# The first norm's factor and offset multiplied into the modulation rows during the mixer, on two partitions, instead of on full tiles at its end

## The chip, the cores and the metric

The kernel runs on one core of a Trainium2 chip. The metric is the time of one execution in microseconds of device time; lower is better. PE is TensorE, DVE is VectorE, ACT is ScalarE, POOL is GpSimd, and SP is SyncE, which here only issues DMAs.

## The reference, cut to what matters

One step of a two-layer diffusion backbone with 128 context tokens and 256 latent tokens of 1024 channels. Each layer has a token mixer (convolution, attention and spatial gating, merged and projected) and a mixture of experts. Both are modulated by rows that come from the conditioning, and each is followed by a layer norm:

```python
def trunk_layer(x, cvec, w_ada, b_ada, mix_params, ln1_g, ln1_b, moe_params, ln2_g, ln2_b, ctx_k, ctx_v):
    m = (jax.nn.silu(cvec) @ w_ada + b_ada)[:, None, :]
    sh1, sc1, g1, sh2, sc2, g2 = jnp.split(m, 6, axis=-1)
    mix, k, v = token_mixer(x * (1 + sc1) + sh1, *mix_params, ctx_k, ctx_v)
    x = layer_norm(ALPHA * x + g1 * mix, ln1_g, ln1_b)
    y = hier_moe(x * (1 + sc2) + sh2, *moe_params)
    x = layer_norm(ALPHA * x + g2 * y, ln2_g, ln2_b)
    return x, k, v
```

The change concerns the input of `hier_moe`. With n the normalised value before factor and offset, it is (n * ln1_g + ln1_b) * (1 + sc2) + sh2, which is n * G + B with G = ln1_g * (1 + sc2) and B = ln1_b * (1 + sc2) + sh2. There are two sets of modulation rows: one for the latent tokens (s = 0) and one for the context tokens (s = 1).

## The kernel before

All 384 tokens are worked on together, as three tiles of 128. For each layer the mixer (`mixer`) walks through 72 pieces of 128x1024 weights, n = 0 to 71. A piece is loaded by SP, split into a high and a low part (ACT line 102 and DVE line 110; a few of the low parts on POOL, also line 110), and multiplied three times on PE, high by high, high by low and low by high (lines 97 to 99, or 488 to 490 for the last pieces). Beside the pieces run side steps, written as generators: the convolution (line 505 on DVE, 31 taps), the gating, the attention in four pairs of heads, and the modulation (`ada`). One step of each is traced per piece.

`ada(l, g)` works out 2048 of the 6144 modulation columns. Its matmuls (line 219) are spread over four steps, one in every fourth piece, with a `yield` after each. Two more steps follow: ACT copies the result, and then it is transposed to columns for other uses (lines 229 to 231), the bias is added (line 243, DVE, 128x512, of which only two partitions in each 32 hold rows), for g = 2 one is added to the scale rows (line 245), and four DMAs on POOL's queue store the rows to the tensor `m_d` in HBM (line 247, 4 KB each). g = 1 gives the gate rows g1 and the shift rows sh2, g = 2 the scale rows sc2 and the gate rows g2. In layer 0 the steps of g = 1 begin at piece 5 and those of g = 2 at piece 21; the last step of g = 2 is traced around piece 34. `br` is a table with the biases in the same layout.

The program is ordered by a planner, which simulates the engines and lays down the order of the instructions on each; only stretches marked as a manual schedule keep the order of the text. Each engine, SP and POOL with their DMA issues among them, then works through its own instructions in that order and waits at the first one whose input is missing.

At the end of the mixer `open_ln1` opens new buffers and loads rows, broadcast over 128 partitions, from SP's queue (lines 889 to 893): g1, the norm's factor `lg` and offset `lb`, and sc2 and sh2 for both sets. Then three products and sums of 128x1024 follow on POOL for each set, line 911 (sc * lb), line 912 (sh + that) and line 913 (sc * lg), so that `rows["sc2.."]` holds G and `rows["sh2.."]` holds B. `lg` and `lb` themselves are used once more, far behind, in `affine` (line 1596).

The output projection of the mixer, pieces 64 to 71, runs at the same time. For each block of 256 columns and each token tile, `ln1_part` multiplies by g1 (line 946, DVE), adds the residual (line 949, DVE) and takes the norm's statistics (line 952, DVE); `logit_tr` transposes the result on PE (line 963) and `logit_mm` multiplies it with the router's weights (line 970). In `last_col` the norm is ended: `mean` (line 999, DVE) multiplies by G and `bias` (line 1002, DVE) adds B. Routing and the experts follow. Line 839 (DVE) is the merge of the first branch: it reads the result of a piece from PSUM and so gives the bank back to PE. Line 621 (POOL) turns the queries by the cosine in the attention, and line 599 (POOL) is a product of the gating branch. Line 332 is the load of a piece or of expert weights.

Of the kernel before, what the change touches and what calls it, by code (L numbers as in the profile page):

```python
# [8 lines left out]
F32 = mybir.dt.float32  # L9
# [5 lines left out]
ALU = mybir.AluOpType  # L15
# [5 lines left out]
D = 1024  # L21
# [58 lines left out]
class Kern:  # L80
# [130 lines left out]
    def ada(self, l, g):  # L211

        nc, a = self.nc, self.a
        ps = self.bank("ms")
        for kp in range(4):
            for k in range(2):
                w = self.get(("a", l, g, kp, k))
                for t in range(4):
                    nc.tensor.matmul(ps[32 * t:32 * t + 32, :], self.cT[:, 2 * kp + k, :],  # L219
                                     w[:, t * 512:t * 512 + 512],  # L220
                                     start=(kp == 0 and k == 0), stop=(kp == 3 and k == 1))
                self.done()
            yield
        sb = self.mix.tile([128, 512], F32, tag="tmp", name="adasb", bufs=3)
        self.act(sb, ps, AF.Copy)
        yield
        p2 = self.bank("ms")
        for j in range(4):
            nc.tensor.transpose(p2[:, j * 128:(j + 1) * 128], sb[:, j * 128:(j + 1) * 128], self.ident)
        mT = self.mT[l]  # L230
        nc.vector.tensor_tensor(
            mT[:, g * 16:(g + 1) * 16, :].rearrange("p (t j) s -> p j t s", j=4),
            p2.rearrange("p (j t r) -> p j t r", j=4, t=4)[:, :, :, 0:2],
            self.bT[:, l, g * 16:(g + 1) * 16].rearrange("p (t j) -> p j t", j=4)
            .unsqueeze(3).to_broadcast([128, 4, 4, 2]),
            op=ALU.add)
        if g != 1:
            j = 8 if g == 0 else 32
            nc.vector.tensor_scalar(mT[:, j:j + 8, :], mT[:, j:j + 8, :], 1.0, None, op0=ALU.add)
        if g > 0:  # L240
            br = self.mix.tile([128, 512], F32, tag="tmp", name="adabr", bufs=3)
            nc.sync.dma_start(br, a["badar"][l * 2 + g - 1])
            nc.vector.tensor_tensor(sb, sb, br, op=ALU.add)
            if g == 2:
                nc.vector.tensor_scalar(sb[0:64, :], sb[0:64, :], 1.0, None, op0=ALU.add)
            for t in range(4):
                nc.gpsimd.dma_start(self.m_d[l][g - 1, :, t * 512:(t + 1) * 512], sb[32 * t:32 * t + 2, :])
        yield
# [627 lines left out]
    def open_ln1(self, l):  # L876
        nc, a = self.nc, self.a
        self.pools.close()
        self.pools = ExitStack()
        P = lambda name, **k: self.pools.enter_context(self.tc.tile_pool(name=f"{name}{l}", reuse_waits="tile", **k))  # L880
        self.wx = P("wx", bufs=4)
        self.mo = P("mo", bufs=1)
        self.lpools = ExitStack()
        self.lp = self.lpools.enter_context(self.tc.tile_pool(name=f"lp{l}", bufs=1, reuse_waits="tile"))
        self.route_consts(l)
        rows = self.rows = {}
        md = self.m_d[l]

        def load(name, src, pool):
            t = pool.tile([128, 1024], F32, tag=name if pool is self.lp else "row", name=name, bufs=1 if pool is self.lp else 2)  # L890
            nc.sync.dma_start(t, src.to_broadcast([128, 1024]))
            rows[name] = t
            return t

        self.r = self.hp.tile([128, NT, D], F32, tag="H", name="r1")
        for s in (1, 0):
            load(f"g1{s}", md[0, s:s + 1, 0:1024], self.lp)
        xs = [self.wx.tile([128, 2, D], F32, tag="wx", name="xs") for _ in range(2)]
        self.xs = [xs[0][:, 0], xs[0][:, 1], xs[1][:, 0]]
        src = a["x"] if l == 0 else self.x_d  # L900
        nc.sync.dma_start(xs[0], src[0:256, :].rearrange("(i p) c -> p i c", p=128))
        nc.sync.dma_start(xs[1][:, 0], src[256:T, :])
        g = load("lg", a["ln"][l * 4:l * 4 + 1, :], self.mo)
        b = load("lb", a["ln"][l * 4 + 1:l * 4 + 2, :], self.mo)
        for s in range(2):
            load(f"sc2{s}", md[1, s:s + 1, 0:1024], self.lp)
            load(f"sh2{s}", md[0, s:s + 1, 1024:2048], self.lp)
        for s in range(2):
            sc, sh = rows[f"sc2{s}"], rows[f"sh2{s}"]
            t = self.lp.tile([128, D], F32, tag="t", name="rtmp", bufs=2)  # L910
            nc.gpsimd.tensor_tensor(t, sc, b, op=ALU.mult)  # L911
            nc.gpsimd.tensor_tensor(sh, sh, t, op=ALU.add)
            nc.gpsimd.tensor_tensor(sc, sc, g, op=ALU.mult)
        self.st1 = self.sm.tile([128, NT, 4, 6], F32, tag="st1", name="st1", bufs=1)

    def route_consts(self, l):
# [1056 lines left out]
```

## Time and profile before

| | before |
|---|---|
| median of 3 runs | 1128.73 us (1127.07 to 1132.06) |
| the profiled execution | 1127.33 us, span 1125.6 us |
| PE busy | 1011.2 us, 90% |
| DVE busy | 810.7 us, 72% |
| ACT busy | 417.4 us, 37% |
| POOL busy | 269.7 us, 24% |

The span runs from the first to the last instruction of the profiled execution; the time is a little longer. Layer 0's mixer lies at about 0 to 405 us and layer 1's at about 600 to 950 us, each followed by its experts. Busy shares are means over all of it; what a single edit is worth is read from the waits in its own stretch. In the views a wait is given in brackets behind the instruction that waited, with what ended it.

### The profile page before, as it was taken

What the parts mean: (1) busy time and instruction counts of PE and PEld (TensorE: products, weight loads), DVE (VectorE), ACT (ScalarE), POOL (GpSimd) and SP (SyncE); (2) the same over time, 40 slices, a digit from 0 to 9 for tenths busy, and PEclk for the clock granted to TensorE, in tenths of its full rate; (3) what the DMA queues carried; (4) which work ended last, traced back from release to release, by engine and by line L of the source; (5) the groups of instructions that cost most, each with busy time, mean ns of one, the idle gap of its engine ahead of it and who ended that gap; (6) DMA issues with size and microseconds to landing.
All of it is one profiled execution on the core that took longest, in us unless ns stands there. A gap on an engine that the chain in (4) does not pass through costs nothing. (4 is left out here: it accounts for less than half of the span.)

```text
span 1125.6 us, 20806 instructions
## 1 busy us (share of the span) xinstructions
PE 1011.2 (90%) x8182; PEld 840.7 (75%) x8182; DVE 810.7 (72%) x1530; ACT 417.4 (37%) x753; POOL 269.7 (24%) x232
## 2 busy tenths in 40 slices
PE   7999999999999999776689998999999999778673
PEld 5898978877999988433259897788999998754322
DVE  4399999965446986762569999997834587777437
ACT  4324254434333324341163443445532341434221
POOL 0001431221100510333244043114111025013335
PEclk9999999999999989897989999999999999989888
DMA  9967668447436667799585756773223666689955
GB/s 358 412 241 257 266 217 294 178 163 270 151 112 246 259 262 293 303 420 403 219 315 201 280 217 233 251 290 127 110 94 132 224 244 229 227 317 416 419 204 194
DMA packets 55101, 282.75 MB, mean 251 GB/s; under 512 B 8060, under 2 KB 12284, under 8 KB 27857
## 3 DMA queue, kind: packets, MB, share of 16 engines
q1 hardware_dynamic: 49632, 270.01, 63.1%
q0 software_dynamic: 5360, 11.29, 2.7%
q8 instruction: 69, 1.13, 0.4%
q14 instruction: 40, 0.32, 0.1%
HBM read 262.13 MB, written 24.71 MB: 255 GB/s over the span
## 5 line engine op out<-in xcount | busy, mean ns | idle before, releaser
L97 PE MATMUL ps_mm<-hThi,wr 128*128 128x384 f32 x672 | 229.9, 343 | 4.4 <-ACT hThi L102 2.3
L110 DVE TENSOR_TENSOR wr<-w_raw,wr 128x1024 fp32r<-128x1024 f32 x124 | 162.2, 1309 | 92.4 <-ACT wr L102 92.3
L98 PE MATMUL ps_mm<-hTlo,wr 128*128 128x384 f32 x672 | 228.0, 340 | 0.6 <-DVE hTlo L441 0.4
L99 PE MATMUL ps_mm<-hThi,wr 128*128 128x384 f32 x672 | 227.5, 339 | 0.6 <-DVE wr L110 0.6
L102 ACT ACTIVATE wr<-w_raw 128x1024 fp32r<-128x1024 f32 x140 | 147.5, 1055 | 68.1 <-PE ps_mm L99 37.8
L505 DVE SCALAR_TENSOR_TENSOR cacc<-pad,par,cacc 128x399 f32<-128x399 f32 x240 | 169.2, 705 | 4.2
L97 PEld LDWEIGHTS ps_mm<-hThi,wr 128*128 128x128 f32 x672 | 127.1, 189 | 18.2 <-issue 4.0
L98 PEld LDWEIGHTS ps_mm<-hTlo,wr 128*128 128x128 f32 x672 | 127.1, 189 | 6.3 <-DVE hTlo L441 2.5
L99 PEld LDWEIGHTS ps_mm<-hThi,wr 128*128 128x128 f32 x672 | 127.2, 189 | 2.5 <-DVE wr L110 0.9
L110 POOL TENSOR_TENSOR wr<-w_raw,wr 128x1024 fp32r<-128x1024 f32 x10 | 24.5, 2447 | 201.6 <-ACT wr L102 201.2
L1458 POOL DMA_INDIRECT y_d<-ys,dst x28 | 28.4, 1016 | 172.3 <-DVE hv L1400 73.3
L1446 PE MATMUL ps_sc<-w,hidT 128*32 128x512 f32 x256 | 43.1, 766 | 28.6 <-ACT ys L102 21.9
L1415 PE MATMUL ps_mm<-hv,win 128*32 128x128 f32 x1024 | 46.4, 277 | 9.2 <-DVE hv L1400 7.8
L1400 DVE COPY hv<-w_raw 128x512 f32 x60 | 41.9, 737 | 16.6 <-PE ps_mm L1415 10.8
L1415 PEld LDWEIGHTS ps_mm<-hv,win 128*32 128x32 f32 x1024 | 35.8, 112 | 22.7 <-DVE hv L1400 12.0
L1409 PE MATMUL ps_mm<-w_raw,win 128*32 128x256 f32 x640 | 47.8, 391 | 3.5 <-ACT win L102 3.5
L219 PE MATMUL ps_ms<-w_raw,cT 128*32 128x512 f32 x320 | 48.7, 612 | 1.4 <-DMA w_raw<-in_wada 1.4
L102 ACT ACTIVATE gate<-ps_mm 128x384 f32<-128x384 f32 x40 | 19.6, 490 | 81.6 <-PE ps_mm L99 80.5
L1446 PEld LDWEIGHTS ps_sc<-w,hidT 128*32 128x32 f32 x256 | 8.2, 123 | 45.8 <-ACT ys L102 32.9
L911 POOL TENSOR_TENSOR rtmp<-sc,lb 128x1024 f32<-128x1024 f32 x4 | 9.8, 2478 | 121.8 <-DMA lb<-in_ln 121.8
L842 POOL TENSOR_TENSOR merged<-merged,gate 128x384 f32<-128x384 f32 x16 | 18.1, 1135 | 87.0 <-DVE gate L841 87.0
L102 ACT ACTIVATE win<-xT 128x256 f32 x64 | 21.5, 409 | 37.6 <-PE ps_mm L1409 30.2
(505 smaller groups left out, 2355.7 us busy)
## 6 DMA issues: line engine op xcount, KB each, us to landing
w_raw<-in_wst SPq DMA_DIRECT2D x68, 1024.0 KB, 6.4
w_raw<-in_wada SPq DMA_DIRECT2D x48, 1024.0 KB, 5.4
w_raw<-in_w SPq DMA_DIRECT2D x40, 1024.0 KB, 10.7
w<-in_w SPq DMA_DIRECT2D x32, 1024.0 KB, 12.3
w_x<-in_w SPq DMA_DIRECT2D x24, 1024.0 KB, 11.8
bias<-in_bias SPq DMA_DIRECT2D x8, 768.0 KB, 7.6
y_d<-zero SPq DMA_DIRECT2D x2, 3072.0 KB, 15.1
yy<-y_d SPq DMA_DIRECT2D x6, 1024.0 KB, 7.1
```

Source lines behind the costliest of these rows:

```text
L97: mm(out, whi, xhi, start=first, stop=False)
L98: mm(out, whi, xlo, start=False, stop=False)
L99: mm(out, wlo, xhi, start=False, stop=last)
L102: return self.nc.scalar.activation(out, in_, f, **k)
L110: (eng or self.nc.vector).tensor_tensor(lo, x, hi.bitcast(F32), op=ALU.subtract)
L219: nc.tensor.matmul(ps[32 * t:32 * t + 32, :], self.cT[:, 2 * kp + k, :], w[:, t * 512:t * 512 + 512], start=(kp == 0 and k == 0), stop=(kp ...
L505: nc.vector.scalar_tensor_tensor(acc, pad[:, j:j + W], w, acc, op0=ALU.mult, op1=ALU.add)
L1400: nc.vector.tensor_copy(hv[:, i, :], src)
L1409: nc.tensor.matmul(ps[e * 32:(e + 1) * 32, 0:256], x[:, k, e * 32:(e + 1) * 32], w[:, e, kk, :], start=k == 0, stop=k == 7, skip_group_che ...
L1415: nc.tensor.matmul(ps[t * 32:(t + 1) * 32, 256:384], x[:, k, 128 + i * 32:160 + i * 32], hv[:, i, kk, h * 128:(h + 1) * 128], start=False, ...
L1446: nc.tensor.matmul(po[e * 32:(e + 1) * 32, :], hT[:, e * 32:(e + 1) * 32], w2[:, e, :], start=True, stop=True)
L1458: ins = nc.gpsimd.indirect_dma_start(out=view, out_offset=bass.IndirectOffsetOnAxis(ap=dst, axis=0), in_=rows, in_offset=None, bounds_chec ...
```

## The change

The three products and sums on POOL for each set, lines 907 to 913, are taken out of `open_ln1`. In their place `ada` works out G and B for g = 2 before the rows are stored. When g = 2 begins, three buffers of 64x512 are taken, and six DMAs from POOL's queue load the norm's factor and offset (each row to two partitions) and the shift rows that g = 1 stored. In its last step, four matmul steps later, DVE does six instructions of 2x512, B = lb * sc + sh and G = sc * lg for each half of the 1024 channels, and POOL's queue stores B over the shift rows in `m_d`. The stores of the scale rows then carry G. The loads in `open_ln1` are the same as before and bring G and B.

```diff
--- before.py
+++ after.py
@@ -211,6 +211,14 @@
     def ada(self, l, g):
 
         nc, a = self.nc, self.a
+        if g == 2:
+            lg, lb, sh = (self.mix.tile([64, 512], F32, tag="lnr", name="lnr", bufs=3) for _ in range(3))
+            for t in range(2):
+                c = slice(t * 512, (t + 1) * 512)
+                r = slice(32 * t, 32 * t + 2)
+                for k, x in enumerate((lg, lb)):
+                    nc.gpsimd.dma_start(x[r, :], a["ln"][l * 4 + k:l * 4 + k + 1, c].to_broadcast([2, 512]))
+                nc.gpsimd.dma_start(sh[r, :], self.m_d[l][0, :, 1024 + t * 512:1024 + (t + 1) * 512])
         ps = self.bank("ms")
         for kp in range(4):
             for k in range(2):
@@ -242,7 +250,14 @@
             nc.sync.dma_start(br, a["badar"][l * 2 + g - 1])
             nc.vector.tensor_tensor(sb, sb, br, op=ALU.add)
             if g == 2:
+
                 nc.vector.tensor_scalar(sb[0:64, :], sb[0:64, :], 1.0, None, op0=ALU.add)
+                for t in range(2):
+                    r = slice(32 * t, 32 * t + 2)
+                    nc.vector.tensor_tensor(lb[r, :], lb[r, :], sb[r, :], op=ALU.mult)
+                    nc.vector.tensor_tensor(lb[r, :], lb[r, :], sh[r, :], op=ALU.add)
+                    nc.vector.tensor_tensor(sb[r, :], sb[r, :], lg[r, :], op=ALU.mult)
+                    nc.gpsimd.dma_start(self.m_d[l][0, :, 1024 + t * 512:1024 + (t + 1) * 512], lb[r, :])
             for t in range(4):
                 nc.gpsimd.dma_start(self.m_d[l][g - 1, :, t * 512:(t + 1) * 512], sb[32 * t:32 * t + 2, :])
         yield
@@ -900,17 +915,11 @@
         src = a["x"] if l == 0 else self.x_d
         nc.sync.dma_start(xs[0], src[0:256, :].rearrange("(i p) c -> p i c", p=128))
         nc.sync.dma_start(xs[1][:, 0], src[256:T, :])
-        g = load("lg", a["ln"][l * 4:l * 4 + 1, :], self.mo)
-        b = load("lb", a["ln"][l * 4 + 1:l * 4 + 2, :], self.mo)
+        load("lg", a["ln"][l * 4:l * 4 + 1, :], self.mo)
+        load("lb", a["ln"][l * 4 + 1:l * 4 + 2, :], self.mo)
         for s in range(2):
             load(f"sc2{s}", md[1, s:s + 1, 0:1024], self.lp)
             load(f"sh2{s}", md[0, s:s + 1, 1024:2048], self.lp)
-        for s in range(2):
-            sc, sh = rows[f"sc2{s}"], rows[f"sh2{s}"]
-            t = self.lp.tile([128, D], F32, tag="t", name="rtmp", bufs=2)
-            nc.gpsimd.tensor_tensor(t, sc, b, op=ALU.mult)
-            nc.gpsimd.tensor_tensor(sh, sh, t, op=ALU.add)
-            nc.gpsimd.tensor_tensor(sc, sc, g, op=ALU.mult)
         self.st1 = self.sm.tile([128, NT, 4, 6], F32, tag="st1", name="st1", bufs=1)
 
     def route_consts(self, l):
```

## Rows read from the trace of the kernel before

**Rows 1.** Busy us of PE, PEld, DVE, ACT, POOL; PEclk, DMA share, GB/s, two stretches.

```profile
220.00:260.00 40.00, 38.49 (x238) 31.95 (x237) 29.15 (x55) 18.98 (x38) 12.92 (x10) 1.00 0.42 151
300.00:340.00 40.00, 40.00 (x233) 40.00 (x232) 19.27 (x27) 12.89 (x16) 4.05 (x4) 1.00 0.35 117
```

**Rows 2.** Timeline of POOL, layer 0: start, duration, instruction, idle before.

```profile
376.02 4.92 POOL L911 TENSOR_TENSOR rtmp<-sc,lb 128x1024 f32<-128x1024 f32 x2 [60.39 <-DMA lb<-in_ln]
...
389.28 2.58 POOL L913 TENSOR_TENSOR sc<-sc,lg 128x1024 f32<-128x1024 f32 x1
```

**Rows 3.** Timeline of DVE, layer 0: first use of the products.

```profile
402.19 1.28 DVE L999 SCALAR_TENSOR_TENSOR t<-r,nmean,sc 128x1024 f32<-128x1024 f32 x1
```

**Rows 4.** Timeline of DVE, layer 0: around the products' start.

```profile
373.93 0.42 DVE L949 SCALAR_TENSOR_TENSOR r<-xs,r 128x256 f32<-128x256 f32 x1
...
374.93 1.22 DVE L110 TENSOR_TENSOR wr<-w_raw,wr 128x1024 fp32r<-128x1024 f32 x1
...
376.40 2.30 DVE L949 SCALAR_TENSOR_TENSOR r<-xs,r 128x256 f32<-128x256 f32 x1
...
379.72 1.51 DVE L949 SCALAR_TENSOR_TENSOR r<-xs,r 128x256 f32<-128x256 f32 x1
...
382.05 1.71 DVE L949 SCALAR_TENSOR_TENSOR r<-xs,r 128x256 f32<-128x256 f32 x1
...
384.13 2.96 DVE L110 TENSOR_TENSOR wr<-w_raw,wr 128x1024 fp32r<-128x1024 f32 x1
```

**Rows 5.** Waits of PE, 376 to 392 and 922 to 939 us.

```profile
PE ps_mm L963 <- DVE r L949: 1.3, 1, 1.3
PE ps_tp L963 <- DVE r L949: 0.8, 1, 0.8
...
PE ps_mm L963 <- DVE r L949: 0.7, 1, 0.7
```

**Rows 6.** Line 247, the stores of modulation rows: issue and landing.

```profile
L247 POOL DMA_DIRECT2D m_d<-adasb x16: 518/533/797, 122.5 to 773.4; - x16
...
DMA to landing us min/median/max: 1.6/1.6/4.6
```

**Rows 7.** Timeline of DVE, layer 0: end of the second modulation step.

```profile
213.94 0.68 DVE L243 TENSOR_TENSOR adasb<-adasb,adabr 128x512 f32<-128x512 f32 x1
214.54 1.10 DVE L505 SCALAR_TENSOR_TENSOR cacc<-pad,par,cacc 128x399 f32<-128x399 f32 x1
...
217.85 0.41 DVE L245 TENSOR_SCALAR adasb<-adasb 64x512 f32<-64x512 f32 x1
...
228.46 0.54 DVE L839 SCALAR_TENSOR_TENSOR merged<-gate,ps_mm 128x384 f32<-128x384 f32 x1
```

**Rows 8.** Timeline of PE, layer 0: its wait in that stretch.

```profile
229.05 0.44 PE L97 MATMUL ps_mm<-hThi,wr 128*128 128x384 f32 x1 [1.51 <-DVE merged L839]
```

**Rows 9.** Timelines of DVE and PE, layer 1: the same place.

```profile
781.23 0.56 DVE L839 SCALAR_TENSOR_TENSOR merged<-gate,ps_mm 128x384 f32<-128x384 f32 x1 [0.67 <-PE ps_mm L99]
...
783.79 0.33 PE L97 MATMUL ps_mm<-hThi,wr 128*128 128x384 f32 x1
```

**Rows 10.** Timeline of POOL, layer 0: its weight piece.

```profile
219.94 2.40 POOL L110 TENSOR_TENSOR wr<-w_raw,wr 128x1024 fp32r<-128x1024 f32 x1 [0.36 <-issue]
```

**Rows 11.** Timeline of POOL, layer 0: the start of the second step.

```profile
133.31 1.32 POOL L599 TENSOR_TENSOR gmt<-gmt,u 128x384 f32<-128x384 f32 x1 [7.86 <-DVE gmt L595]
...
140.75 1.06 POOL L621 TENSOR_TENSOR q<-q,rope 128x256 f32<-128x256 f32 x1
```

**Rows 12.** Timeline of PE at 148 us; then PEclk from there on.

```profile
148.24 0.53 PE L97 MATMUL ps_sc<-qkh 64*128 64x384 f32 x2 [1.78 <-ACT qkh L102]
...
148.00:152.00 4.00, 3.76 (x15) 2.64 (x16) 3.96 (x9) 2.20 (x5) 1.57 (x2) 0.57 0.42 173
```

**Rows 13.** Timeline of SP; then the DMA share of a later stretch.

```profile
387.12 0.33 SPq L332 DMA_DIRECT2D w_raw<-in_w  x1
...
392.00:396.00 4.00, 4.00 (x36) 4.00 (x36) 1.85 (x5) 0.38 (x1) 0.00 (x0) 1.00 0.00 0
```

## The prediction

> **What bounds the kernel now.** I read the page's table of engines first, then the busy time by stretch, then the waits of PE, then the timelines of POOL and DVE around the two places that the change touches. In the mixer of each layer PE is the bound: from 300 to 340 us it is busy all the time at full clock [rows 1], and PE loses time there only where it waits for one named instruction. So an edit in the mixer is worth what it does to such a wait, and the same work on DVE or POOL elsewhere is worth nothing.
>
> Three of those waits matter. At the end of the mixer PE waits for DVE's line 949, 1.3 and 0.8 us in layer 0 and 0.7 us in layer 1 [rows 5]. These fall while POOL runs the six row products that the change removes: in layer 0 they start at 376.02 and end at 391.86 [rows 2]. Nobody waits for the products themselves, since DVE takes the first at 402.19 [rows 3], ten microseconds later. What they do is slow DVE: line 949 takes 0.42 us just before and 2.30, 1.51 and 1.71 us beside them, and the weight split of line 110 takes 2.96 us instead of 1.22 [rows 4]. The third wait is in the middle of the mixer, where the second modulation step ends: PE waits 1.51 us at 229.05 for line 839 [rows 8], which DVE reaches at 228.46 [rows 7]. DVE has not one gap before that from 213.94 on, so there it is DVE that sets PE's pace. This is where the change adds DVE work.
>
> **The change part by part.** Removed: six products of 128x1024 on POOL per layer, 15.8 us of POOL [rows 2]. As nobody waits for them, the gain is what they cost DVE, and of that only the part for which PE waits: 1.3 + 0.8 + 0.7 = 2.8 us [rows 5]. I take it whole: these are all the waits of PE that the view names in those stretches. The bounds are 0 (another input of the same transposes is late next) and, beyond that, the rival on DVE below. The loads of factor, offset, scale and shift rows stay on SP's queue in the same number and order. The shift rows now wait for a store at the end of the second modulation step, more than 100 us earlier (217.85 against 376.02, [rows 7, 2]), which has landed after at most 4.6 us [rows 6]: nothing.
>
> Added on POOL at the start of the second step: six loads of 2x512 per layer. The nearest row is line 247, a DMA of the same 4 KB from the same queue: 533 ns of POOL each (518 to 797) [rows 6], so 6 x 0.53 = 3.2 us, with bounds of 3.1 and 4.8. What hides it is a gap: POOL stands idle for 7.86 us before line 599 at 133.31 [rows 11], which is where the second step begins. The loads of the shift rows wait for the stores of the first step; those land in 1.6 us, 4.6 at worst [rows 6]. I cost this at nothing. If the cover is gone, the instructions queued behind the loads are lines 599 and 621, on which the attention, and PE with it, depends (second rival). That the data comes in time needs no cover: 4.6 us at worst [rows 6] against the 80 us from 133.31 to 213.94 [rows 11, 7].
>
> Added on DVE at the end of that step: four products and two sums of 2x512, six instructions per layer. No row has two partitions. The nearest is line 243, a sum of the same 512 columns over 128 partitions: 0.68 us, and the next instruction starts 0.60 us after it [rows 7]. Six of these are 6 x 0.60 = 3.6 us. The bounds: 6 x 0.41 = 2.5, if they run like line 245 on half the partitions, and 6 x 1.10 = 6.6, if each meets POOL as line 505 does at 214.54 [rows 7].
>
> Who pays for it? In layer 0 the six become ready after line 245, at 217.85, and line 839 comes at 228.46 with DVE full between [rows 7]; the time from line 243 to line 245, which depends on it, is 3.9 us, so a chain three deep ends by about 226 and lies ahead of line 839 whole, or nearly. PE already waits for line 839 [rows 8], so there is no slack: +3.6 us, with bounds of 0 (the six come behind line 839) and 6.6. In layer 1 DVE is idle for 0.67 us before line 839, and the line ends at 781.23 + 0.56 = 781.79, while PE wants the bank only at 783.79 [rows 9]: 2.0 us of slack. Shifted by 3.6 - 0.67 = 2.9 us, it costs 2.9 - 2.0 = 0.9 us, with bounds of 0 and 6.6 - 0.67 - 2.0 = 3.9.
>
> Two stores per layer are also added on POOL, 2 x 0.53 = 1.1 us [rows 6], and the two stores of the scale rows wait longer, for the last product. Queued behind them on POOL is the weight split that now runs from 219.94 to 222.34 [rows 10]. PE takes that piece at 229.05 [rows 8]: 6.7 us of slack. With the chain ending near 226, four stores of 2.1 us and the split of 2.40, it would be ready at about 230.5, and by then PE is waiting for line 839 until 229.0 + 3.6 = 232.6 anyway. Nothing more, then; but were the six instructions quick and the stores slow, this would be what is late next.
>
> The sum: -2.8 + 3.6 + 0.9 = +1.7 us. The profiled execution took 1127.33 us (span 1125.6), so by its own time 1129.0. The median of the runs, 1128.73, is 1.4 us above the profiled execution, and against that it is 1130.4. I put the forecast between the two, at 1129.7.
>
> **The rivals.** A measurement of this kernel can tell about 0.5%, 5.6 us, from no change.
>
> First, the gain without the price. The order on DVE is the planner's, and it may place the six instructions behind line 839, where PE needs nothing of DVE at once. Then only -2.8 is left: 1127.33 - 2.8 = 1124.5, still within 0.5%. For it speaks that the planner mixes other work into chains (3.9 us from line 243 to 245, [rows 7]); against it, that everything the six need is there at 217.85, ten microseconds before line 839.
>
> Second, the slower side: POOL's queue at the start of the step. The gap of 7.86 us closes at 133.31, and line 621, which turns the queries, stands at 140.75 [rows 11]. PE waits at 148.24 for what follows from it, 1.78 us already [rows 12], so there is no slack. If the six loads are queued not in the gap but right ahead of line 621, all 3.2 us go to PE, in both layers: +1.7 + 6.4 = +8.1, 1135.4 us. It decides from the point where the last load ends after 140.75, that is, when the first starts later than 137.5. Against it: the step begins before that, and the loads need nothing that is late.
>
> Third, the faster side: DVE's lost time counts whole. Up to the end of the split of line 110 DVE loses 1.88 + 1.09 + 1.29 + 1.74 = 6.0 us beside POOL [rows 4], and SP issues a load of expert weights only then, at 387.12 [rows 13]. If it is these loads that set the start of the expert stage, both layers gain up to 6.0 us, and -12.0 + 3.6 + 0.9 = -7.5 gives 1119.8. Against it: from 392 to 396 us the DMA engines stand still [rows 13], so the load was not what the next ones waited for. The Trainium skill, "SBUF — State Buffer", section "Who interferes with whom", says that a DVE instruction with two SBUF inputs and a GpSimd instruction that reads SBUF take turns, the later one being blocked until the first is done. The trace agrees that they get in each other's way, 2.30 us against 0.42 [rows 4]; it does not show that the blocked time is on the path.
>
> Fourth, the clock. After the wait of 1.78 us at 148.24 the granted clock of the four microseconds was 0.57, between the levels of 1.2 and 2.4 GHz [rows 12]; over the stretch with the wait of 1.51 it stayed at 1.00 [rows 8, 1]. A wait of 1.51 + 3.6 = 5.1 us may end at the lower level: 4 us at 0.57 lose 1.7 us, and the sum becomes +3.4, 1130.7 us on the profiled execution.
>
> **How the numbers follow.** Forecast 0.42, gain without price 0.25, POOL's queue 0.14, DVE's whole time 0.09, clock 0.10. Faster by over 0.5% is the third rival, 0.09; slower the second, 0.14; the other three are within 0.5%, 0.77. The range goes from the first rival's 1124.5, less the 1.66 by which the lowest run lies under the median, 1123, up to the second rival's 1135.5; beyond it lie the third rival and the upper bounds of the added DVE work.
>
> **What would show it.** Right: line 949 takes 0.4 us to the end and the waits for it are gone; six new DVE instructions of about 0.6 us stand ahead of line 839 in layer 0; PE's wait there is near 5 us; the loads stand in POOL's gap. Wrong: PE's wait for line 839 stays at 1.5 us, the wait at 148 us grows, or the expert stage starts earlier by more than PE gained.

## The result, and the profile after

The changed kernel takes 1145.86 us (median of 4 runs, 1143.65 to 1146.83), the kernel before beside it 1130.23 us (1127.07 to 1132.06). The ratio is 1.0139, 95% interval 1.0108 to 1.017: slower by 1.4%, some 16 us. The forecast was 1129.7 us and its range ended at 1135.5. The profiled execution took 1146.83 us, span 1145.0, against 1127.33 and 1125.6. It is the slowest of the four, and that of before lies near the fastest, so the spans differ by 19.4 us where the medians differ by 15.6.

In the listing after the change, line 839 of before is line 854, 949 is 958, 999 is 1008, 110 is still 110; the six new DVE instructions are lines 257 to 259, the new loads lines 220 and 221, the stores of B line 260.

**What was removed pays about as forecast, by the trace.** The first fence is DVE's timeline of the kernel after at the end of layer 0's mixer (start, duration, instruction).

```profile
381.21 0.42 DVE L958 SCALAR_TENSOR_TENSOR r<-xs,r 128x256 f32<-128x256 f32 x1
...
383.68 0.40 DVE L958 SCALAR_TENSOR_TENSOR r<-xs,r 128x256 f32<-128x256 f32 x1
...
390.10 1.23 DVE L110 TENSOR_TENSOR wr<-w_raw,wr 128x1024 fp32r<-128x1024 f32 x1 [1.75 <-ACT wr L102]
...
406.91 1.28 DVE L1008 SCALAR_TENSOR_TENSOR t<-r,nmean,sc 128x1024 f32<-128x1024 f32 x1
```

Line 958 takes 0.4 us to the end where it took up to 2.30 [rows 4], and no wait of PE for it is left, in either layer [rows 5]. Line 1008 starts at 406.91, 4.7 us later than before [rows 3], but the first multiplication by g1 came 7.3 us later (379.40 against 372.12): in between 2.6 us were won. In layer 1 it is 1.1 us (from +16.1 to +15.0).

**The loss lies in the middle of both mixers.** The next two fences give one row for the same stretch of each layer in both kernels: from the second merge before the change's place (lines 839 and 854), in layer 1 from the last one before it, to the first merge of the second branch (lines 841 and 856). The columns are length, busy us of PE, PEld, DVE, ACT and POOL with the number of instructions, granted clock, DMA share and GB/s. First the kernel before, then after.

```profile
202.60:273.90 71.30, 68.43 (x421) 55.60 (x419) 53.48 (x109) 31.43 (x63) 17.25 (x16) 1.00 0.50 183
757.00:821.00 64.00, 63.17 (x365) 54.85 (x363) 45.92 (x96) 31.43 (x63) 17.75 (x16) 1.00 0.30 109
```

```profile
202.20:281.20 79.00, 75.03 (x421) 58.04 (x419) 55.51 (x115) 31.44 (x63) 18.24 (x18) 0.98 0.44 165
762.80:837.10 74.30, 68.90 (x374) 59.10 (x372) 53.34 (x105) 32.14 (x64) 18.14 (x18) 0.95 0.27 98
```

The stretch of layer 0 is 7.7 us longer, that of layer 1 10.3, together 18.0 of the 19.4 us by which the spans differ. (The rest is small change of both signs: the 3.7 us won at the mixers' ends, 4.4 us lost from the end of layer 1's mixer to the end of the span, behind everything that the change touches, and less than 1 us elsewhere.) How much of it PE stands idle can be read off: 79.00 - 75.03 = 4.0 us against 2.9 before, and 74.30 - 68.90 = 5.4 against 0.8. In layer 0 PE has as many instructions as before, 421, and is busy with them for 6.6 us more. In layer 1 it is busy for 5.7 us more, but nine more instructions fall into the stretch.

Of the 2.9 us of idle time before in layer 0, 1.4 are a wait for a load of modulation weights (line 219, at 271.85). None of the kernels with added work has this wait; the forecast did not count it. So the stretch of a kernel that has the added work far behind it (the one with the six late, below) is a fairer measure of what the change lost in layer 0, 9.1 us:

```profile
201.50:271.40 69.90, 68.39 (x421) 55.61 (x419) 53.52 (x109) 31.46 (x63) 17.25 (x16) 1.00 0.50 189
```

What filled these two places, layer by layer:

Layer 0 first. DVE's timeline of the kernel after:

```profile
220.08 3.08 DVE L257 TENSOR_TENSOR lnr<-lnr,adasb 2x512 f32<-2x512 f32 x2
223.19 0.75 DVE L681 TENSOR_SCALAR s<-s,se 128x384 f32<-128x384 f32 x2
...
225.29 0.67 DVE L258 TENSOR_TENSOR lnr<-lnr 2x512 f32<-2x512 f32 x1
...
227.51 0.68 DVE L259 TENSOR_TENSOR adasb<-adasb,lnr 2x512 f32<-2x512 f32 x1
...
229.91 0.55 DVE L854 SCALAR_TENSOR_TENSOR merged<-gate,ps_mm 128x384 f32<-128x384 f32 x1
```

PE's timeline of the kernel after, behind that:

```profile
230.51 0.69 PE L97 MATMUL ps_mm<-hThi,wr 128*128 128x384 f32 x1 [3.38 <-DVE merged L854]
230.99 0.52 PE L98 MATMUL ps_mm<-hTlo,wr 128*128 128x384 f32 x1
```

And two windows of the kernel after (columns as above):

```profile
228.00:232.00 4.00, 1.49 (x5) 1.49 (x6) 3.97 (x10) 0.28 (x1) 0.61 (x2) 0.80 0.02 2
232.00:236.00 4.00, 4.00 (x21) 3.96 (x20) 1.57 (x3) 0.00 (x0) 3.33 (x3) 0.78 0.32 92
```

The six stand ahead of line 854, as forecast. The first two take 3.08 us together, beside POOL's weight split, which runs from 219.51 for 2.40 us; the other four take 0.67 or 0.68. Line 854 starts 1.45 us later than line 839 did [rows 7], and PE waits 3.38 us where it waited 1.51 [rows 8]. Behind this wait the clock falls: the windows show 0.80 and 0.78 (1.00 is the level of 2.4 GHz, 0.50 that of 1.2), and a matmul of 384 columns takes 0.52 us instead of the 0.33 that it takes before the wait. Before, the same stretch ran at 1.00 [rows 1].

Layer 1, the same views of the kernel after: DVE's timeline,

```profile
780.66 1.39 DVE L257 TENSOR_TENSOR lnr<-lnr,adasb 2x512 f32<-2x512 f32 x2
...
786.80 0.67 DVE L258 TENSOR_TENSOR lnr<-lnr 2x512 f32<-2x512 f32 x1
...
788.71 1.76 DVE L259 TENSOR_TENSOR adasb<-adasb,lnr 2x512 f32<-2x512 f32 x1
...
791.11 1.50 DVE L110 TENSOR_TENSOR qkh<-q,qkh 128x256 fp32r<-128x256 f32 x1
792.53 1.34 DVE L110 TENSOR_TENSOR qkh<-k,qkh 128x384 fp32r<-128x384 f32 x1
793.79 0.54 DVE L854 SCALAR_TENSOR_TENSOR merged<-gate,ps_mm 128x384 f32<-128x384 f32 x1
```

POOL's timeline there, and in the kernel before the two splits of line 110 in the same place on DVE,

```profile
791.30 2.15 POOL L534 TENSOR_TENSOR ctot<-ctot,csq 128x384 f32<-128x384 f32 x2
```

```profile
777.88 0.41 DVE L110 TENSOR_TENSOR qkh<-q,qkh 128x256 fp32r<-128x256 f32 x1
778.22 0.54 DVE L110 TENSOR_TENSOR qkh<-k,qkh 128x384 fp32r<-128x384 f32 x1
```

PE's timeline of the kernel after,

```profile
788.82 0.44 PE L97 MATMUL ps_mm<-gmhi,wr 128*128 128x384 f32 x1 [1.02 <-ACT gate L102]
...
794.38 0.69 PE L97 MATMUL ps_mm<-hThi,wr 128*128 128x384 f32 x1 [3.19 <-DVE merged L854]
```

and the windows.

```profile
792.00:796.00 4.00, 1.61 (x5) 1.62 (x6) 4.00 (x6) 0.35 (x1) 1.37 (x2) 0.70 0.00 0
796.00:800.00 4.00, 4.00 (x15) 4.00 (x14) 1.72 (x3) 0.00 (x0) 0.00 (x0) 0.50 0.34 74
```

Line 854 starts at 793.79, 12.6 us later than line 839 [rows 9], when the layer had begun only some 6 us later. The six take 5.2 us together, the last of them 1.76. The two splits of line 110 ahead of line 854 take 1.50 and 1.34 us beside POOL's line 534, where the kernel before, with the same two ahead of its merge, takes 0.41 and 0.54. DVE has no idle time in front of it, where it had 0.67 us, and PE, which did not wait for it at all, now waits 3.19 us, and 1.02 us for ACT before that. Again the clock falls behind the wait, to 0.70 and 0.50.

### The profile page after: what moved, and what is told of

The parts are those of the page before. It is cut to its first block, busy times and chain, and to the rows that moved or that the text cites. A ratio compares the mean times of both kernels' runs of the same rounds, so it can differ in the third digit from the quotient of the medians.

```text
span 1145.0 us, 20842 instructions
## 1 busy us (share of the span) xinstructions
PE 1024.1 (89%) x8182; PEld 848.4 (74%) x8182; DVE 811.6 (71%) x1542; ACT 417.2 (36%) x753; POOL 248.8 (22%) x236
## 5 line engine op out<-in xcount | busy, mean ns | idle before, releaser
L97 PE MATMUL ps_mm<-hThi,wr 128*128 128x384 f32 x672 | 232.5, 347 | 9.8 <-DVE merged L854 6.6
L110 DVE TENSOR_TENSOR wr<-w_raw,wr 128x1024 fp32r<-128x1024 f32 x124 | 159.9, 1290 | 106.2 <-ACT wr L102 106.1
L99 PE MATMUL ps_mm<-hThi,wr 128*128 128x384 f32 x672 | 229.7, 342 | 0.7 <-DVE wr L110 0.7
L97 PEld LDWEIGHTS ps_mm<-hThi,wr 128*128 128x128 f32 x672 | 128.6, 192 | 23.2 <-DVE merged L854 7.5
L99 PEld LDWEIGHTS ps_mm<-hThi,wr 128*128 128x128 f32 x672 | 128.5, 191 | 4.7 <-DVE wr L110 2.2
L1409 DVE COPY hv<-w_raw 128x512 f32 x60 | 49.7, 870 | 17.5 <-PE ps_mm L1424 13.5
```

The lines of the kernel that those rows point to most:

```text
L97: mm(out, whi, xhi, start=first, stop=False)
L99: mm(out, wlo, xhi, start=False, stop=last)
L110: (eng or self.nc.vector).tensor_tensor(lo, x, hi.bitcast(F32), op=ALU.subtract)
L1409: nc.vector.tensor_copy(hv[:, i, :], src)
```

## The experiments

All ratios are to the kernel before in the same series. Shifts are those of corresponding instructions in the profiled executions, against the kernel before.

**The two halves of the change.** The first leaves out the products and puts nothing in their place (factor and offset of the norm are missing from its result).

```diff
-        for s in range(2):
...
-            nc.gpsimd.tensor_tensor(t, sc, b, op=ALU.mult)
-            nc.gpsimd.tensor_tensor(sh, sh, t, op=ALU.add)
-            nc.gpsimd.tensor_tensor(sc, sc, g, op=ALU.mult)
```

> The removal alone: the six products on POOL are gone from open_ln1 and nothing takes their place, so factor and offset of the norm are left out of the expert input. The order of all instructions on PE, DVE and ACT is that of before. Both theories (DVE time, and the planner's order) expect the gain by itself: line 949 back at 0.4 us everywhere, the waits of 2.1 us in layer 0 and 0.7 us in layer 1 gone, so 2.8 us less than before, ratio about 0.9975. If the products had cost nothing on the path, 1.000.

The second is the changed kernel with the products kept as well (factor and offset are applied twice).

```diff
-        load("lg", a["ln"][l * 4:l * 4 + 1, :], self.mo)
-        load("lb", a["ln"][l * 4 + 1:l * 4 + 2, :], self.mo)
+        g = load("lg", a["ln"][l * 4:l * 4 + 1, :], self.mo)
+        b = load("lb", a["ln"][l * 4 + 1:l * 4 + 2, :], self.mo)
...
+            nc.gpsimd.tensor_tensor(t, sc, b, op=ALU.mult)
+            nc.gpsimd.tensor_tensor(sh, sh, t, op=ALU.add)
+            nc.gpsimd.tensor_tensor(sc, sc, g, op=ALU.mult)
```

> The addition alone: loads, six DVE instructions and stores of the change in the modulation step, and the six products on POOL kept at the end of the mixer (so factor and offset are applied twice). The order on PE, DVE and ACT is that of the changed kernel. Both theories expect the whole loss here, and more than in the change by what the removal gives: 15.6 + 2.8 = 18.4 us over before, ratio about 1.016. If instead the loss came from the removal, about 1.000.

Measured: removal alone 1125.24 us, ratio 0.9994 (0.9976 to 1.0011); addition alone 1147.28 us, 1.0172 (1.0141 to 1.0204), some 19 us. By time the removal cannot be told from no change; by the trace it wins 2.5 us at the end of layer 0's mixer and 1.1 in layer 1's. So by the trace the gain is near its forecast, 3.6 us against 2.8, and it is the addition that cost 19 us where 4.5 were forecast.

**The change without its six DVE instructions**: loads, buffers and stores stay, and the stores write what was loaded (factor and offset are left out of the result).

```diff
-                    nc.vector.tensor_tensor(lb[r, :], lb[r, :], sb[r, :], op=ALU.mult)
-                    nc.vector.tensor_tensor(lb[r, :], lb[r, :], sh[r, :], op=ALU.add)
-                    nc.vector.tensor_tensor(sb[r, :], sb[r, :], lg[r, :], op=ALU.mult)
```

> The change with its loads and stores from POOL, in its place, but without the six DVE instructions (factor and offset of the norm are left out, the offset is stored in place of the shift). The order on PE is that of before through layer 0. Theory DVE time: the loads and stores cost nothing, ratio 0.9975 as for the removal alone. Rival POOL's queue: if the six loads and two more stores are what costs, layer 0 loses the 7 us between pieces 36 and 42 here too, and the whole is about +10 us.

Measured: 1124.81 us, 0.9969 (0.9946 to 0.9991). PE's wait for the merge is 1.5 us as before. The loads and stores on POOL's queue cost nothing; the whole loss comes with the six instructions, or with the order that the planner lays round them.

**The six on POOL instead of DVE.**

```diff
-                    nc.vector.tensor_tensor(lb[r, :], lb[r, :], sb[r, :], op=ALU.mult)
+                    nc.gpsimd.tensor_tensor(lb[r, :], lb[r, :], sb[r, :], op=ALU.mult)
...
```

> Right for all outputs. The change with the six instructions on POOL in place of DVE. The planner's order on PE is nearly that of the changed kernel (it differs from that of before in 46 places). Theory DVE time: line 854 comes no later than in before, so the wait for it stays near 1.5 us and the clock up; POOL needs about 1.3 us for each of the six, 8 us in a row, and the weight split behind them has 6.7 us of slack, so between -2.8 and +3 us, ratio 0.997 to 1.003. Theory order: the loss comes with the order, so it stays at +10 us or more, ratio over 1.009.

Measured: 1141.65 us, 1.0132 (1.0098 to 1.0165), no better. The number is the one expected if the order were the cause, but the other expectation, that line 854 comes no later, did not hold, so this run does not part the two. POOL's timeline of this kernel, layer 0:

```profile
217.77 3.75 POOL L257 TENSOR_TENSOR lnr<-lnr,adasb 2x512 f32<-2x512 f32 x2 [2.10 <-DVE se L679]
...
225.88 2.54 POOL L259 TENSOR_TENSOR adasb<-adasb,lnr 2x512 f32<-2x512 f32 x1
```

DVE's beside it:

```profile
221.04 3.17 DVE L681 TENSOR_SCALAR s<-s,se 128x384 f32<-128x384 f32 x2
...
228.69 2.74 DVE L681 TENSOR_SCALAR s<-s,se 128x384 f32<-128x384 f32 x2
```

PE's, and then a window:

```profile
233.76 0.69 PE L97 MATMUL ps_mm<-hThi,wr 128*128 128x384 f32 x1 [6.75 <-DVE merged L854]
```

```profile
232.00:236.00 4.00, 2.24 (x7) 2.24 (x8) 4.00 (x6) 0.00 (x0) 3.91 (x7) 0.50 0.03 4
```

On POOL an instruction of 2x512 takes 1.3 to 2.5 us, and DVE's line 681, which in the kernel after takes 0.75 us for two, takes 3.17 and 2.74 beside it. So line 854 comes still later, PE waits 6.75 us and the clock goes to 0.50. The Trainium skill, "SBUF — State Buffer", section "Who interferes with whom", says that a `tensor_scalar` on DVE can run in a mode that uses the port pair it shares with GpSimd, and that of the two the one issued later is blocked until the other is done. As far as the rows go this trace agrees: 0.75 us against 3.17 and 2.74.

**Half the instructions in the same place**: both halves of the channels in one instruction of 64x512, three in all.

```diff
+                nc.vector.tensor_tensor(lb, lb, sb[0:64, :], op=ALU.mult)
+                nc.vector.tensor_tensor(lb, lb, sh, op=ALU.add)
+                nc.vector.tensor_tensor(sb[0:64, :], sb[0:64, :], lg, op=ALU.mult)
```

> Right for all outputs. The change with half the DVE time in the same place: both halves of the rows in one instruction of 64x512, so three instructions of 0.6 us per layer in place of six (the loads fill all 64 partitions; the tile of the shift rows is set to zero first on POOL). Theory DVE time: the loss follows the DVE time ahead of line 854, and half of it, 1.8 us, gives half of the 18 us or less, +0 to +6 us against before with the gain of the removal. Theory order: the planner's order is again another one than before, and the loss is as in the change, +15 us, or what that order happens to cost.

Measured: 1129.56 us, 1.0007 (0.9988 to 1.0027). PE waits 0.9 us for the merge in layer 0 and the clock stays at 1.00. In layer 0 the three take 2.39, 0.67 and 0.68 us, 3.7 together, the six of the change 5.8. The three cost about 4 us more than none (1.0007 against 0.9969), the six some 19: the loss is not in proportion. It lies within the 0 to 6 us expected of DVE's time.

**The rows folded as 128x16**: the rows are stored as before the change, read back in that shape, three DVE instructions, stored again.

```diff
+            rows = [self.mix.tile([128, 16], F32, tag="lnr", name="lnr", bufs=4) for _ in range(4)]
...
+            nc.vector.tensor_tensor(lb, lb, sc, op=ALU.mult)
+            nc.vector.tensor_tensor(lb, lb, sh, op=ALU.add)
+            nc.vector.tensor_tensor(sc, sc, lg, op=ALU.mult)
```

> Right for all outputs. The same fold, but the rows lie as 128x16 (loaded from and stored to m_d after the rows were stored), so DVE has three instructions of about 0.16 us in place of six of 0.6 us per layer. The planner nevertheless lays down another order on PE, DVE and ACT, nearly that of the changed kernel. Theory DVE time (the 3.6 us of DVE ahead of line 854 and what the clock loses behind that wait): the loss goes with the DVE time, 0.5 us instead of 3.6, so about -2 us against before, ratio 0.998. Theory order (the other order of the side work costs by itself): most of the 18 us stays, +10 to +15 us against before, ratio 1.009 to 1.013.

The same fold, tied behind the products of the second branch (pieces 48 and on):

```diff
+        with self.tc.issue_after(self.pin_v):
+            nc.vector.tensor_tensor(lb, lb, sc, op=ALU.mult)
+            nc.vector.tensor_tensor(lb, lb, sh, op=ALU.add)
+            nc.vector.tensor_tensor(sc, sc, lg, op=ALU.mult)
```

> Right for all outputs. The fold of 128x16 again, but its loads, three DVE instructions and stores are tied behind a product of the second branch, pieces 48 and on, where DVE is idle half of the time. The order on PE and ACT is exactly that of before, on DVE too but for the three. Both theories expect the gain of the removal and nothing else: -2.8 us, ratio 0.9975. Together with p1 it tells them apart: the same instructions, only the order differs.

Measured: 1124.22 us, 0.9979 (0.996 to 0.9997), and 1124.89 us, 0.997 (0.9951 to 0.999). The first one's instructions on PE stand in another order than those of the kernel before in many places, about as many as in the kernel after; the second one's stand in that of before. So this other order costs nothing that can be measured; that of the kernel after is not tried by itself. In layer 0 of the first, the three take 0.17, 0.17 and 1.27 us, and the planner put them behind the merge (228.52 against 227.20), so this run does not show what little DVE work ahead of it costs.

**The change's own six instructions, late**: six DVE instructions of 2x512 with their loads and stores, tied behind the products of the second branch. The scale rows, stored as before the change, are read back for it.

```diff
+        with self.tc.issue_after(self.pin_v):
+            for t in range(2):
+                r = slice(32 * t, 32 * t + 2)
+                nc.vector.tensor_tensor(lb[r, :], lb[r, :], sc[r, :], op=ALU.mult)
+                nc.vector.tensor_tensor(lb[r, :], lb[r, :], sh[r, :], op=ALU.add)
+                nc.vector.tensor_tensor(sc[r, :], sc[r, :], lg[r, :], op=ALU.mult)
```

> Right for all outputs. The change's own loads of 2x512, its six DVE instructions of 2x512 per layer and its stores, but tied behind products of the second branch (pieces 48 and on), where DVE is idle half of the time; the scale rows are read back from m_d. The order on PE and ACT is exactly that of before. Theory DVE time: what counts is where the 3.6 us stand, and here PE waits for nothing behind them, so only the gain of the removal is left, -2 to -3.5 us, ratio 0.9975. Theory of the instructions themselves (two partitions from partition 32 on, 512 long, or the DMAs of 4 KB from POOL are bad wherever they stand): most of +15 us stays.

Measured: 1122.64 us, 0.9952 (0.9932 to 0.9972), faster than both kernels. DVE's timeline of this kernel in layer 0, and the window around it:

```profile
311.93 2.10 DVE L269 TENSOR_TENSOR lnr<-lnr 2x512 f32<-2x512 f32 x2
...
317.11 0.67 DVE L271 TENSOR_TENSOR lnr<-lnr 2x512 f32<-2x512 f32 x1
```

```profile
312.00:316.00 4.00, 4.00 (x25) 4.00 (x24) 3.94 (x6) 0.84 (x3) 1.39 (x1) 1.00 0.49 205
```

Here too two of the six are stretched (2.10 us), and PE does not notice: it is busy for all 4.00 us at full clock. It is the place that costs, with the order that the planner lays round it, and not the work: here the instructions on PE keep the order of before.

**Each layer by itself.** One kernel has layer 0 as in the change and layer 1 late, the other the reverse.

```diff
-        if g == 2:
+        if g == 2 and l == 0:
...
+            if n == 49 and l != 0:
+                self.side.append(self.fold_rows(l))
```

> In layer 0 the modulation step is the change's own (six DVE instructions in its last step); in layer 1 the same six are tied late, behind the products of the second branch. Theory A (each layer pays at its own place): layer 0's part of the loss alone, 5.7 us at the start of layer 1 in the trace of the changed kernel, on top of the kernel with both late (0.995): ratio 1.000 to 1.003, and layer 1's mixer as long as with both late. Theory B (what happens in layer 1 is the echo of layer 0): nearly the whole loss is here, 1.010 to 1.014. My forecast's own sizes would give 0.995 + 3.6 us = 0.998.

> The reverse: late in layer 0, the change's own place in layer 1. PE's order is that of the kernel before through the whole of layer 0. Theory A: layer 1's part alone, about 13 us on top of the kernel with both late: ratio 1.005 to 1.008, with a wait of PE for the merge of the first branch in layer 1 of about 3 us, and the clock below full behind it. Theory B: 0.995 to 0.998. My forecast's own size for layer 1, 0.9 us, would give 0.996.

Measured: 1133.35 us, 1.0022 (1.0007 to 1.0036), and 1133.71 us, 1.0034 (1.0013 to 1.0055). Over the kernel with both late that is 0.0070 and 0.0082, together 0.0152; the change is 0.0187 over it. The intervals are wide enough for the two to add up. Layer 0 alone shows the shift of the kernel after to the tenth (+7.3 us at the first merge of the second branch), and no wait for the merge in layer 1. From the second kernel, layer 1, the list of PE's waits (us in total, times, longest) and two windows:

```profile
PE ps_mm L97 <- DVE merged L883: 4.0, 1, 4.0
```

```profile
784.00:788.00 4.00, 2.21 (x7) 2.21 (x8) 4.00 (x8) 0.00 (x0) 2.12 (x3) 0.61 0.01 1
788.00:792.00 4.00, 4.00 (x15) 4.00 (x14) 0.46 (x2) 0.00 (x0) 0.00 (x0) 0.54 0.73 262
```

The order of PE is that of before through the whole of layer 0 here, and layer 1 still has the wait, 4.0 us, with the clock at 0.61 and 0.54 behind it. So layer 1's loss is its own, not an echo of layer 0's. It came out below what I expected of that layer (1.005 to 1.008), by time; in the trace its stretch is longer by 12.6 us (76.60 against 64.00). Layer 0 bears out the expected 1.000 to 1.003.

**The six right behind the merge** instead of ahead of it, in the same region of both mixers; loads, stores and rows are those of the kernel with the six late.

```diff
+                        self.pin_v = nc.vector.scalar_tensor_tensor(m, g, 1.0, pss[b][:, :T], op0=ALU.add, op1=ALU.mult).ins
...
+            if n == 36:
+                self.side.append(self.fold_rows(l))
```

> The six DVE instructions in both layers in the same region of the mixer, but tied right behind a merge of the first branch instead of offered ahead of it; loads, stores and rows as in the kernel with the six late. Theory A (what costs is the delay of that merge, with the clock behind it): PE's wait there is no longer than in the kernel before (1.5 us), ratio 0.995 to 0.999. Rival (any six DVE instructions in this region cost the same, since DVE has no gap there and what follows is pushed behind and laid in another order): 1.008 to 1.014.

Measured: 1131.14 us, 1.0006 (0.9986 to 1.0026), between the two theories. PE's timeline of this kernel in layer 0, at its wait:

```profile
231.88 0.45 PE L97 MATMUL ps_mm<-hThi,wr 128*128 128x384 f32 x1 [1.51 <-DVE merged L867]
```

The window behind the wait and the whole stretch of layer 0, as above:

```profile
232.00:236.00 4.00, 4.00 (x26) 3.97 (x27) 3.94 (x8) 0.17 (x1) 0.22 (x1) 1.00 0.16 27
204.70:280.20 75.50, 73.40 (x425) 56.49 (x423) 56.91 (x115) 31.42 (x64) 22.36 (x24) 1.00 0.47 177
```

The wait is 1.51 us as before and the clock stays at 1.00, yet the stretch of layer 0 is 75.50 us long, 4.2 more than before and 5.6 more than with the six late. This part of the loss does not come from a longer wait or a lower clock. Most of it is seen in one group of PE's lines, the modulation's matmuls in that stretch (busy us and mean ns): of this kernel, of the kernel before and of the kernel after.

```profile
L219 PE MATMUL ps_ms<-w_raw,cT 128*32 128x512 f32 x62 | 11.2, 603 | 0.0
```

```profile
L219 PE MATMUL ps_ms<-w_raw,cT 128*32 128x512 f32 x62 | 7.9, 600 | 1.4 <-DMA w_raw<-in_wada 1.4
```

```profile
L227 PE MATMUL ps_ms<-w_raw,cT 128*32 128x512 f32 x62 | 11.0, 602 | 0.0
```

PE's timeline of the kernel after, one of these groups:

```profile
254.34 1.04 PE L227 MATMUL ps_ms<-w_raw,cT 128*32 128x512 f32 x2
256.03 1.92 PE L227 MATMUL ps_ms<-w_raw,cT 128*32 128x512 f32 x14
```

The same 62 matmuls of 600 ns keep PE busy for 7.9 us before, 11.0 after and 11.2 here. They have 32 columns of weights each, and several run side by side if they follow each other: 14 take 1.92 us. Where the planner lays others between them the group is begun twice: 2 of the 16 take 1.04 us by themselves and the 14 behind them still 1.92. As I read it, DVE's work behind the merge (the convolution's pads, the attention) comes later, and what depends on it falls among these matmuls.

## Why the prediction was wrong

**The gain** (-2.8): right in its mechanism and near in size by the traces, 2.6 and 1.1 us in that of after, 2.5 and 1.1 with the removal alone; the times do not show it (0.9994).

**Loads and stores on POOL** (nothing): right. The loads of the shift rows start at 125.89, in the gap; those of factor and offset were laid further ahead, from 2.5 us on. PE's wait at 148 us is 1.84 against 1.78 [rows 12], and the kernel without the six DVE instructions loses nothing. The rival of POOL's queue fell.

**DVE's whole lost time**: fell. The end of the mixer gains little more than what PE had waited, 2.6 us against 2.1 in layer 0 and 1.1 against 0.7 in layer 1, and not 6.0.

**The gain without the price**: the six were not laid behind the merge; but it is what happens when they are put late, 0.9952, and better than the -2.8 us it was given.

**The six on DVE** (+3.6 in layer 0, +0.9 in layer 1, with bounds up to 6.6 and 3.9): this is the step that failed. Its place was right, its size was not, nor its bounds: 7.7 and 10.3 us. The working took PE's wait to grow by DVE's added time less its slack and left all the rest as it was; its premise, that an edit in the mixer is worth what it does to PE's waits, does not hold here. The runs show in its place:

- The wait itself grew by less than I said, in layer 0 from 1.51 to 3.38, not to 5.1. DVE's six took 5.8 us, not 3.6, but the planner put other DVE work behind the merge: the pads stand at 231.89, behind it, where before they stood at 224.90, ahead of it. As I read it, this deferred work is what came back later.
- The clock, my fourth rival, did fall, and in both layers. By the windows it costs at most (0.20 + 0.22) x 4 = 1.7 us in layer 0, the rival's own figure though behind another wait than it took, which is luck, and (0.30 + 0.50) x 4 = 3.2 in layer 1, where I had not thought of it since I saw no wait there. It was treated as a case beside the forecast, but it hangs on the forecast's own longer wait and belonged in its sum. One wait does not decide it, though: at 148 us the kernel after waits 1.84 us and its window shows 1.00, where before the same wait, 1.78 us, was followed by 0.57 [rows 12]. PE's timeline of the kernel after there, and the window:

```profile
148.44 0.45 PE L97 MATMUL ps_sc<-qkh 64*128 64x384 f32 x2 [1.84 <-ACT qkh L102]
```

```profile
148.00:152.00 4.00, 2.75 (x17) 2.03 (x18) 3.96 (x9) 2.35 (x5) 1.65 (x2) 1.00 0.49 198
```

- PE's own work got longer. Of the 6.6 us in layer 0, 3.1 are the broken groups of line 227 and 1.7 the clock; the remaining 1.8 I put down to the attention's small matmuls, most of whose groups are some tenths longer. The kernel with the six behind the merge shows 4.2 us of this kind with the wait and the clock as before.
- In layer 1 DVE came to the merge 6.7 us later, not 2.9: from the bias sum to the merge it took 18.54 us (775.25 to 793.79) against 11.81 (769.42 to 781.23). The pads and the two splits stood ahead of the merge before as well. New there are the six, 5.2 us instead of 3.6, and the 1.9 us by which the splits grew beside POOL. Less the slack of 2.0 us that is 4.7, near the 4.2 us of waits that PE then has; so the slack was read rightly, and the time on DVE was not. Up to 3.2 us of clock come on top. Of the rest of the 10.3 us, nine more matmuls in the stretch, 0.17 us apart, make 1.6.

What stays open: the shares of wait, clock and PE's own work are read off traces and not tried one by one. The runs do not part them in layer 1, where the six behind the merge cost 1.6 us and ahead of it 10.3, and what makes one changed order dear (after) and another free (the 128x16 fold) is read from the traces, not tried by itself. Nor was the further 4.4 us behind layer 1's mixer in the profiled execution followed up; the other kernels here shift by -1.2 to +4.8 us there, among them the one without the six instructions by +3.8.

## What to carry to other kernels

Where one engine paces another with no gap, added work on the pacing engine costs more than its own duration: price the clock behind the longer wait and what is pushed back into the next stage, and take the added instructions and their neighbours at what they last beside the third engine, not alone. Small work with a deadline far off should be tied to a stretch where the bounding engine waits for nobody; the change with its six instructions in one place made the kernel 1.4% slower, with the same six in another 0.5% faster. And before costing a move at its durations, look at which matmuls run side by side only because they are adjacent.

## What the runs showed of the hardware

- Length of PE's wait and granted clock of the windows of 4 us in which it ends and behind: 1.51 us, 1.00; 1.84 us, 1.00, but 1.78 us in the same place of the kernel before, 0.57 [rows 12]; 3.38 us, 0.80 and 0.78; 3.19 us with 1.02 us some five microseconds earlier, 0.70 and 0.50; 4.00 us, 0.61 and 0.54; 6.75 us, 0.50.
- An instruction on two partitions takes DVE as long as one on 128: 0.67 us for 2x512, 0.68 for 128x512 [rows 7]. On POOL 2x512 takes 1.3 to 2.5 us.
- Matmuls with 32 columns of weights: 14 or 16 in a row in 1.92 us, two alone in 1.04.
